# Weight splits at a higher scheduler priority, and the last head's share last in the first two tiles of the second output product

## The chip, the core and the metric

The kernel runs on one core of one Trainium2 chip. A core has a matrix engine (TensorE, PE in the profile, with its weight loads as PEld), a vector engine (VectorE, DVE), a scalar engine (ScalarE, ACT), GpSimd (POOL) and SyncE (SP), which here issues most DMAs. The metric is the device time of one execution in microseconds.

## The reference

Two blocks of a network, 512 tokens of width 1024, all in float32. Block 1: a hybrid mixer (chunk gating beside a gated delta rule with 4 heads), cross attention to 256 memory tokens, an MLP with squared ReLU. Block 2: a mixer with an mLSTM and a sliding-window attention, an MLP, and a gate with per-layer inputs. What matters here, cut to its core:

```python
h = rmsnorm(x, norm_mix)
y_a = chunk_spatial_gating(gu, gv, ...)             # 512 columns
o = gated_delta_rule(q, k, v, g, beta)              # 4 heads x 128
o = rmsnorm(o, dn_onorm) * silu(gate)
x = x + concatenate([y_a, o]) @ w_out               # w_out: 1024 x 1024
x = x + memory_cross_attention(rmsnorm(x, norm_xa), rmsnorm(mem, norm_mem), ...)
x = x + squared_relu_mlp(rmsnorm(x, norm_mlp), ffn_w1, ffn_w2)
```

## The kernel before

Activations lie feature-major in SBUF: 8 tiles of 128 features x 512 tokens (`x`, x_fm in the profile). TensorE multiplies float32 operands as two shorter parts, hi and lo: `mm3` issues three matmuls for one product, hi x hi (L276), hi x lo (L277) and lo x hi (L278). In a feature-major product the weights are the fixed operand, 128 x 128, and 512 tokens stream.

Weights come in pieces of 128 x 1024 through `wload` (L249): a DMA on SP into a raw buffer (wr, 2 of them), a cast to hi on ScalarE (L257, wh) and a subtraction raw − hi on VectorE (L258, wl; 3 buffers each of wh and wl). A raw buffer is free for the next DMA when the subtraction has read it, and a wh buffer for the next cast when TensorE has done its last matmul with it. `wgran` loads the two pieces that a product with 1024 rows needs; `w_out_b`, with 512 rows, needs one. In the two MLPs there are extra buffers (wrx, whx, wlx), and there the second product's weights come through `st_weights` and `split_sb` (casts in L318, subtractions in L319), not through `wload`. `split_sb` is also what splits activations: hi on ScalarE (L321 with a scale), lo on VectorE (L322).

No order is written by hand. A scheduler goes through the program once, and puts each engine's instructions into one fixed list by priority and by what is ready in its own plan; the priority goes by the place in the program. On the chip each engine runs its list in that order, and an instruction whose data isn't there holds up the rest of its list.

Four places are spoken of below.

- **The last head** (at about 285 us in the profile). Each delta-rule head ends in `fin`: four transposes (L768, tile c) and a `split_sb` into `yb` (L321, L322). `w_out1` multiplies the four heads' `yb` by `w_out_b`: `g` goes over four pieces of weights, each with two output tiles (PSUM tiles psd), and each tile adds up the four heads, k = 0 to 3 (`proj_fm`). Behind each tile stands `ev`: the residual (L465) and the norm's split and squares.
- **The memory projections** (150 to 285 us). The norm of the memory tokens and the projections `xa_wk` and `xa_wv` run beside the delta rule's heads. The heads' triangular solves are groups of small matmuls (L656) with small rows on VectorE between them.
- **From the first MLP to mixer 2** (765 to 795 us). The MLP's last products end in PSUM tiles x and are added to x_fm (L977). A norm follows: split and squares (L321, L322, L331, L332), the sum over features by matmuls with a column of ones (`tok_rs`: L340 into pss, L342), an inverse root in 11 small rows on VectorE (`rsqrt`, L180 to L185, three Newton steps), a second one, and `tok_bc` (L349 copies, TensorE transposes in L352, ScalarE copies in L354). Mixer 2's first tiles don't need the result in their matmuls, only in their evacuation.
- **From the second MLP to the tail** (1615 to 1640 us). The same norm, with one inverse root.

## Time and profile before

| | us |
|---|---|
| median of 3 runs | 1704.14 (1703.59 to 1705.08) |
| the profiled execution's own time | 1704.19 |
| its span, first to last instruction | 1702.4 |
| TensorE busy | 1678.3 |
| VectorE busy | 1214.9 |
| ScalarE busy | 821.8 |

The times are of whole executions; the profile is of one. What the kernel's trace records lies within the span, and 1.8 us of the execution's time lie around it. A matmul's busy time includes the pipeline's depth, so two matmuls in a row overlap: what one costs is read from the distance of two starts, and what a wait costs from the same distance less the usual one. In a row of the timeline stand the start, the duration, the engine, the line, the operation, out <- in and shape, and in brackets the idle time ahead of it with what ended it. In a row of windows stand the window, its length, busy time of PE, PEld, DVE, ACT and POOL with their counts, the granted clock, the share of the DMA engines and GB/s.

### The profile page before, as it was taken

Reading aid. Unit: us, or ns where it says so; the run is one execution under the profiler, and the core shown is the slowest. Engines: PE = TensorE matmul, PEld = TensorE weight load, DVE = VectorE, ACT = ScalarE, POOL = GpSimd, SP = SyncE. Lnnn points to the kernel's source line nnn. Section 1 sums busy time; section 2 is a strip of 40 time slices with the busy share of each in tenths; the row PEclk is TensorE's granted clock in tenths of the full one; section 3 lists DMA queues with packets and bytes.
Section 4 is the critical chain, followed back from the end, with each engine's and each line's share of the span. In section 5 each row is a group of like instructions: output and inputs, shape, how many; then the busy total and the mean of one; then the engine's idle time right before and its main releaser. Section 6 shows DMA issues by size and latency. Waiting matters only on the chain.

```text
span 1702.4 us, 25975 instructions
## 1 busy us (share of the span) xinstructions
PE 1678.3 (99%) x9924; PEld 1453.7 (85%) x9924; DVE 1214.9 (71%) x2574; ACT 821.8 (48%) x1462; POOL 66.2 (4%) x86
## 2 busy tenths in 40 slices
PE   9999999999999999999999999999999999999998
PEld 8988888887898989898988887788888989898987
DVE  6988885656676768688845569865556767676875
ACT  6365745444444444454444457654244444444553
POOL 0200000000000000000000000000000000000000
PEclk9999999999999999999999999999999999999999
DMA  6321367545545464423333332334464454643331
GB/s 203 100 76 54 94 160 176 136 99 169 124 137 161 136 161 136 124 89 110 101 94 93 100 87 72 90 87 123 112 189 127 133 165 132 166 133 121 100 112 50
DMA packets 81948, 205.64 MB, mean 121 GB/s; under 512 B 13088, under 2 KB 14240, under 8 KB 81824
## 3 DMA queue, kind: packets, MB, share of 16 engines
q1 hardware_dynamic: 62672, 169.29, 31.8%
q0 software_dynamic: 9216, 16.78, 6.7%
q10 hardware_dynamic: 9936, 17.91, 3.8%
q8 instruction: 78, 1.28, 0.3%
q14 instruction: 46, 0.38, 0.1%
HBM read 201.59 MB, written 35.65 MB: 139 GB/s over the span
## 4 chain that ended last, share of the span: by engine, by line
PE 88%; DVE 8%; ACT 2%; issue 1%; DMA 1%; ACTq 0%; DVEq 0%
PE psd L277 21%; PE psd L278 21%; PE psd L276 21%; PE x L276 5%; PE x L277 5%; PE x L278 5%; DVE wl L258 2%; PE c L656 1%; PE c L602 1%; ACT wh L257 1%; PE lg L1338 1%; PE po L1365 1%; DVE acc L332 1%; DVE S L432 1%; PE m L1259 1%
## 5 line engine op out<-in xcount | busy, mean ns | idle before, releaser
L278 PE MATMUL psd<-S,wl 128*128 128x512 f32 (+1 forms) x1256 | 483.9, 386 | 2.6 <-DVE wl L258 2.5
L276 PE MATMUL psd<-S,wh 128*128 128x512 f32 (+1 forms) x1256 | 482.9, 385 | 1.1 <-ACT S L321 1.1
L277 PE MATMUL psd<-S,wh 128*128 128x512 f32 (+1 forms) x1192 | 458.9, 385 | 1.0 <-DVE S L322 0.8
L278 PEld LDWEIGHTS psd<-S,wl 128*128 128x128 f32 x1256 | 236.3, 188 | 48.0 <-DVE wl L258 3.8
L276 PEld LDWEIGHTS psd<-S,wh 128*128 128x128 f32 x1256 | 236.6, 188 | 46.4 <-ACT S L321 1.5
L258 DVE TENSOR_TENSOR wl<-wr,wh 128x1024 fp32r<-128x1024 f32 (+2 forms) x160 | 192.1, 1200 | 115.1 <-ACT wh L257 113.1
L277 PEld LDWEIGHTS psd<-S,wh 128*128 128x128 f32 x1192 | 224.3, 188 | 44.1 <-DVE S L319 1.4
L257 ACT CAST wh<-wr 128x1024 fp32r<-128x1024 f32 (+2 forms) x160 | 163.9, 1026 | 151.5 <-PE psd L277 104.9
L278 PE MATMUL psd<-wh,S 128*128 128x256 f32 (+2 forms) x480 | 135.8, 283 | 0.0
L276 PE MATMUL psd<-wh,S 128*128 128x256 f32 (+2 forms) x480 | 135.6, 283 | 0.0
L277 PE MATMUL psd<-wl,S 128*128 128x256 f32 (+2 forms) x480 | 135.5, 282 | 0.0
L276 PE MATMUL x<-S,wh 128*128 128x256 f32 x452 | 128.0, 285 | 3.3 <-DVE x_fm L977 2.9
L277 PE MATMUL x<-S,wh 128*128 128x256 f32 x452 | 126.4, 281 | 0.0
L278 PE MATMUL x<-S,wl 128*128 128x256 f32 x452 | 126.0, 280 | 0.0
L277 PE MATMUL psd<-S,whx 128*128 128x512 f32 (+1 forms) x296 | 109.0, 368 | 0.1
L276 PE MATMUL psd<-S,whx 128*128 128x512 f32 (+1 forms) x296 | 107.9, 366 | 0.0
L278 PE MATMUL psd<-S,wlx 128*128 128x512 f32 (+1 forms) x296 | 107.1, 362 | 0.0
L977 DVE TENSOR_TENSOR x_fm<-x_fm,x 128x256 f32<-128x256 f32 x192 | 78.8, 416 | 27.2 <-PE x L278 27.0
L276 PEld LDWEIGHTS psd<-wh,S 128*128 128x128 f32 x480 | 90.4, 189 | 0.4
L277 PEld LDWEIGHTS psd<-wl,S 128*128 128x128 f32 x480 | 90.4, 188 | 0.4
L278 PEld LDWEIGHTS psd<-wh,S 128*128 128x128 f32 x480 | 90.5, 188 | 0.1
L276 PEld LDWEIGHTS x<-S,wh 128*128 128x128 f32 x452 | 84.9, 188 | 6.4 <-DVE x_fm L977 3.2
(465 smaller groups left out, 3178.7 us busy)
## 6 DMA issues: line engine op xcount, KB each, us to landing
wrx<-in_ffn_w_dram SPq DMA_DIRECT2D x32, 512.0 KB
wrx<-in_w_up_dram SPq DMA_DIRECT2D x20, 512.0 KB
wr<-in_w_in_qk_dram SPq DMA_DIRECT2D x16, 512.0 KB
sums_ffn_w<-in_ffn_w_dram ACTq DMA_DIRECT2D x32, 256.0 KB
wr<-in_ffn_w_dram SPq DMA_DIRECT2D x16, 512.0 KB
sums_w_down<-in_w_down_dram ACTq DMA_DIRECT2D x32, 256.0 KB
wr<-in_w_in_v_dram SPq DMA_DIRECT2D x12, 512.0 KB
wr<-in_w_up_dram SPq DMA_DIRECT2D x12, 512.0 KB
```

The source lines that it names most:

```text
L257: self.last_cast = nc.scalar.copy(hi[:, c], raw[:, c])
L258: nc.vector.tensor_tensor(out=lo[:, c], in0=raw[:, c], in1=hi[:, c].bitcast(F32), op=ALU.subtract)
L276: mm(ps, ah, bh, start=first, stop=False, skip_group_check=more)
L277: mm(ps, ah, bl, start=False, stop=False, skip_group_check=more)
L278: self.last_mm = mm(ps, al, bh, start=False, stop=last, skip_group_check=more)
L332: nc.vector.tensor_tensor(out=acc, in0=acc, in1=sq, op=ALU.add)
L432: nc.vector.tensor_scalar(out=d, in0=d, scalar1=ag[:, j, 0:1], scalar2=r[:, j:j + 1], op0=ALU.subtract, op1=ALU.mult)
L602: nc.tensor.matmul(blk(ps, b), lhs(b), rhs(b), start=True, stop=True)
L656: nc.tensor.matmul(ps[:, b * n:(b + 1) * n], lhs[:, b], rhs(b), start=True, stop=True)
L977: TT(out=x[n][t], in0=x[n][t], in1=ps, op=op)
L1259: nc.tensor.matmul(pX[:, :W], PT[:, tt], va[:, tt], start=True, stop=True)
L1338: nc.tensor.matmul(ps[:, i, K0:], qs[:, 2 * e2 + i, cs], kd[:, w, kc], start=(w == 0), stop=(w == 1))
```

## The change

The cast and the subtraction of every piece of weights that comes through `wload` get a priority that is higher by 400. The scheduler may so place them earlier in ScalarE's and VectorE's lists; the DMA that fills the raw buffer keeps its own. `split_sb` returns its cast. The cast of the second piece of `w_out_b` (g = 1) must be issued after head 3's cast. In `w_out1` the two tiles of the first piece are opened together: k = 0, 1, 2 of both, then k = 3 of both, then both evacuations. No arithmetic is added or removed.

```diff
@@ -246,7 +246,7 @@
                 lambda: self.t(p, [P, kt, n], "wl" + x, F32R, bufs=b))
 
 
-    def wload(self, src, kt, n, pieces=None):
+    def wload(self, src, kt, n, pieces=None, behind=None):
 
         nc = self.nc
         raw, hi, lo = (f() for f in self.wtiles(kt, n))
@@ -254,18 +254,20 @@
             nc.sync.dma_start(raw[:, c], src[:, c])
             if then:
                 then()
-            self.last_cast = nc.scalar.copy(hi[:, c], raw[:, c])
-            nc.vector.tensor_tensor(out=lo[:, c], in0=raw[:, c], in1=hi[:, c].bitcast(F32), op=ALU.subtract)
+            with self.tc.high_priority(400):
+                with self.tc.issue_after(behind.ins) if behind else nullcontext():
+                    self.last_cast = nc.scalar.copy(hi[:, c], raw[:, c])
+                nc.vector.tensor_tensor(out=lo[:, c], in0=raw[:, c], in1=hi[:, c].bitcast(F32), op=ALU.subtract)
         return hi, lo
 
-    def wgran(self, name, g, n=256, nk=8, pieces=None):
+    def wgran(self, name, g, n=256, nk=8, pieces=None, behind=None):
 
         if self.wx is None:
             self.job()
         src = self.D[name]
         parts = []
         for h in range(nk // 4):
-            parts.append(self.wload(src[g, h], 4, n, pieces if h == 0 else None))
+            parts.append(self.wload(src[g, h], 4, n, pieces if h == 0 else None, behind))
         hi = [parts[k // 4][0][:, k % 4] for k in range(nk)]
         lo = [parts[k // 4][1][:, k % 4] for k in range(nk)]
         return hi, lo
@@ -315,11 +317,12 @@
 
         nc = self.nc
         if scale is None:
-            nc.scalar.copy(hi, src)
+            cast = nc.scalar.copy(hi, src)
             nc.vector.tensor_tensor(out=lo, in0=src, in1=hi.bitcast(F32), op=ALU.subtract)
         else:
-            nc.scalar.activation(hi, src, AF.Copy, scale=scale)
+            cast = nc.scalar.activation(hi, src, AF.Copy, scale=scale)
             nc.vector.scalar_tensor_tensor(out=lo, in0=src, scalar=scale, in1=hi.bitcast(F32), op0=ALU.mult, op1=ALU.subtract)
+        return cast
 
     def sq_acc(self, acc, src, k, scale=None, n=T):
         nc = self.nc
@@ -766,7 +769,7 @@
             psy = psc()
             for b in range(NB):
                 nc.tensor.transpose(blk(psy, b), o[:, b], ident)
-            self.split_sb(yb_h[:, h], yb_l[:, h], psy, self.vec[:, C_ONORM:C_ONORM + 1])
+            self.yb_cast = self.split_sb(yb_h[:, h], yb_l[:, h], psy, self.vec[:, C_ONORM:C_ONORM + 1])
 
         yield fin
 
@@ -780,8 +783,19 @@
             self.add_res(o, ps)
             self.norm_tile(o, xh, xl, acc, "norm_xa")
 
-        for g in range(4):
-            self.proj_fm(self.wgran("w_out_b", g, nk=4), *self.yb, (2 * g, 2 * g + 1), ev)
+
+        wh, wl = self.wgran("w_out_b", 0, nk=4)
+        (yh, yl), ps = self.yb, [self.psd() for _ in range(2)]
+        for ks in ((0, 1, 2), (3,)):
+            for j in range(2):
+                for k in ks:
+                    c = slice(j * P, (j + 1) * P)
+                    self.mm3(ps[j], wh[k][:, c], wl[k][:, c], yh[k], yl[k], k == 0, k == 3)
+        for j in range(2):
+            ev(j, ps[j])
+        for g in range(1, 4):
+            w = self.wgran("w_out_b", g, nk=4, behind=self.yb_cast if g == 1 else None)
+            self.proj_fm(w, *self.yb, (2 * g, 2 * g + 1), ev)
         self.dump("x1", self.x)
         return xh, xl, acc
```

The lines of the rows below are those of each kernel's own file: from `wload` on, a line of the changed kernel is some 2 to 14 higher (L258 becomes L260, L321 and L322 become L323 and L324, L768 becomes L771, L977 becomes L991).

**The last head.** ScalarE's list before, from the scale of head 3's output (do) by its norm. wh_3580 is the second piece of `w_out_b`; S_176_1229 is `yb`, split from the transposed head (c_619_3448); S_592_3235 belongs to the memory projections.

```order
L763 ACTIVATE do_2947<-do_2947,dsc_2996 128x128 x4
L257 CAST wh_3580<-wr_3579 128x1024
L321 ACTIVATE S_176_1229<-c_619_3448,vec 128x512
L321 ACTIVATE S_592_3235<-psd_3496,rsmy_2723 128x256
L219 DMA sums_ffn_w_5_68<-in_ffn_w_dram 128x512
L257 CAST wh_3626<-wr_3625 128x1024
L219 DMA sums_ffn_w_5_68<-in_ffn_w_dram 128x512
```

And of the changed kernel, at the same place:

```order
L766 ACTIVATE do_2947<-do_2947,dsc_2996 128x128 x4
L323 ACTIVATE S_592_3235<-psd_3496,rsmy_2723 128x256
L323 ACTIVATE S_176_1229<-c_619_3448,vec 128x512
L259 CAST wh_3580<-wr_3579 128x1024
L259 CAST wh_3626<-wr_3625 128x1024
L219 DMA sums_ffn_w_5_68<-in_ffn_w_dram 128x512 x2
L323 ACTIVATE S_628_3528<-x_fm,vec 128x512
```

Head 3's cast now stands ahead of the second piece's cast. On TensorE, the list before around head 3's transposes (L768); psd_3496 is the last tile of the memory projections and psd_3541 the first of `w_out1`, with wh_3536 the first piece of `w_out_b`:

```order
L768 MATMUL c_619_3448<-masks,do_2947 128x128
L276 MATMUL psd_3496<-wh_3464,S_477_2660 128x256
L768 MATMUL c_619_3448<-masks,do_2947 128x128
L277 MATMUL psd_3496<-wl_3465,S_477_2660 128x256
L278 MATMUL psd_3496<-wh_3464,S_478_2661 128x256
L276 MATMUL psd_3496<-wh_3464,S_477_2660 128x256
L277 MATMUL psd_3496<-wl_3465,S_477_2660 128x256
L278 MATMUL psd_3496<-wh_3464,S_478_2661 128x256
L276 MATMUL psd_3541<-S_176_1229,wh_3536 128x512
```

and in the changed kernel, where psd_3542 is the second tile of `w_out1`:

```order
L279 MATMUL psd_3541<-S_177_1230,wh_3536 128x512
L771 MATMUL c_619_3448<-masks,do_2947 128x128 x2
L280 MATMUL psd_3541<-S_176_1229,wl_3537 128x512
L771 MATMUL c_619_3448<-masks,do_2947 128x128
L278 MATMUL psd_3541<-S_176_1229,wh_3536 128x512
L771 MATMUL c_619_3448<-masks,do_2947 128x128
L279 MATMUL psd_3541<-S_177_1230,wh_3536 128x512
L280 MATMUL psd_3541<-S_176_1229,wl_3537 128x512
L278 MATMUL psd_3541<-S_176_1229,wh_3536 128x512
L279 MATMUL psd_3541<-S_177_1230,wh_3536 128x512
L280 MATMUL psd_3541<-S_176_1229,wl_3537 128x512
L278 MATMUL psd_3542<-S_176_1229,wh_3536 128x512
```

The transposes have moved from the end of the memory projections into the first products of `w_out1`. Before, five matmuls of psd_3496 and nine of psd_3541 (k = 0 to 2) stand between the last transpose and the first matmul that needs head 3 (k = 3); now it is 14 of the two tiles of `w_out1`, and all six matmuls of k = 3 come behind them.

**From the first MLP to mixer 2.** VectorE's list before, from L342, where the row sums of the norm are read; rsi, rsy and rst are the inverse root's tiles, and wl_8182 is a piece of mixer 2's weights:

```order
L342 TENSOR_SCALAR rsv_8018<-pss_8013 128x4
L258 TENSOR_TENSOR wl_8182<-wr_8180,wh_8181 128x1056
L180 TENSOR_SCALAR rsi_8020<-rsv_8018 128x4
L1202 MEMSET mprev_8494 128x4
L181 TENSOR_SCALAR rsy_8021<-rsi_8020 128x4
L183 TENSOR_TENSOR rst_8022<-rsy_8021 128x4
L184 SCALAR_TENSOR_TENSOR rst_8022<-rst_8022,rsv_8018 128x4
L185 SCALAR_TENSOR_TENSOR rsy_8021<-rst_8022,rsy_8021 128x4
L183 TENSOR_TENSOR rst_8022<-rsy_8021 128x4
L184 SCALAR_TENSOR_TENSOR rst_8022<-rst_8022,rsv_8018 128x4
L185 SCALAR_TENSOR_TENSOR rsy_8021<-rst_8022,rsy_8021 128x4
L183 TENSOR_TENSOR rst_8022<-rsy_8021 128x4
```

and in the changed kernel, where wl_8188 and wl_8303 are the next two pieces:

```order
L260 TENSOR_TENSOR wl_8188<-wr_8186,wh_8187 128x1056
L345 TENSOR_SCALAR rsv_8018<-pss_8013 128x4
L180 TENSOR_SCALAR rsi_8020<-rsv_8018 128x4
L181 TENSOR_SCALAR rsy_8021<-rsi_8020 128x4
L1216 MEMSET mprev_8494 128x4
L183 TENSOR_TENSOR rst_8022<-rsy_8021 128x4
L184 SCALAR_TENSOR_TENSOR rst_8022<-rst_8022,rsv_8018 128x4
L185 SCALAR_TENSOR_TENSOR rsy_8021<-rst_8022,rsy_8021 128x4
L183 TENSOR_TENSOR rst_8022<-rsy_8021 128x4
L184 SCALAR_TENSOR_TENSOR rst_8022<-rst_8022,rsv_8018 128x4
L185 SCALAR_TENSOR_TENSOR rsy_8021<-rst_8022,rsy_8021 128x4
L260 TENSOR_TENSOR wl_8303<-wr_8301,wh_8302 128x1024
```

Before, wl_8188 stands 5 rows behind the last of these and wl_8303 16 rows. wl_8182 has moved up among the squares, wl_8188 stands ahead of the first row of the inverse root, and wl_8303 behind its second Newton step. On TensorE, 10 more matmuls of mixer 2's first two tiles now stand ahead of the MLP's last products, 48 of which follow them instead of 36, and the row sums come later: 25 matmuls lie between the MLP's last product and the first row sum, where there were 20.

**From the second MLP to the tail.** VectorE's list before; x_15919, x_15920 and x_16049 are PSUM tiles of the MLP's second product, and wlx_16163 belongs to the tail's weights:

```order
L977 TENSOR_TENSOR x_fm<-x_fm,x_15920 128x256
L977 TENSOR_TENSOR x_fm<-x_fm,x_16049 128x256
L258 TENSOR_TENSOR wlx_16163<-wr_16161,whx_16162 128x512
L977 TENSOR_TENSOR x_fm<-x_fm,x_15919 128x256
L322 SCALAR_TENSOR_TENSOR S_2480_15755<-x_fm,vec,S_2478_15753 128x512
L332 TENSOR_TENSOR acc_15756<-acc_15756,sq_16015 128x512
L319 TENSOR_TENSOR wl_16046<-wrx_16024,wh_16045 128x1024
L322 SCALAR_TENSOR_TENSOR S_2480_15755<-x_fm,vec,S_2478_15753 128x512
L332 TENSOR_TENSOR acc_15756<-acc_15756,sq_16020 128x512
L977 TENSOR_TENSOR x_fm<-x_fm,psd_16051 128x256
```

and in the changed kernel, with wlx_16185 the tail's next piece:

```order
L991 TENSOR_TENSOR x_fm<-x_fm,x_15920 128x256
L260 TENSOR_TENSOR wlx_16163<-wr_16161,whx_16162 128x512
L991 TENSOR_TENSOR x_fm<-x_fm,x_15919 128x256
L324 SCALAR_TENSOR_TENSOR S_2480_15755<-x_fm,vec,S_2478_15753 128x512
L335 TENSOR_TENSOR acc_15756<-acc_15756,sq_16015 128x512
L324 SCALAR_TENSOR_TENSOR S_2480_15755<-x_fm,vec,S_2478_15753 128x512
L260 TENSOR_TENSOR wlx_16185<-wrx_16183,whx_16184 128x512
L335 TENSOR_TENSOR acc_15756<-acc_15756,sq_16020 128x512
L321 TENSOR_TENSOR wl_16046<-wrx_16024,wh_16045 128x1024
L991 TENSOR_TENSOR x_fm<-x_fm,x_16049 128x256
```

The residual from x_16049 has moved behind a norm's rows and two subtractions. On TensorE the 12 matmuls that write the next part into x_16049 now come after 12 of x_16050.

## The prediction

> **What bounds the kernel now.** I read the page's first part first, then the costliest groups with the idle time ahead of them, then PE's timeline around every wait of more than 0.3 us, and then what stands on DVE and ACT there.
>
> ```profile
> PE 1678.3 (99%) x9924; PEld 1453.7 (85%) x9924; DVE 1214.9 (71%) x2574; ACT 821.8 (48%) x1462; POOL 66.2 (4%) x86
> PEclk9999999999999999999999999999999999999999
> L278 PE MATMUL psd<-S,wl 128*128 128x512 f32 (+1 forms) x1256 | 483.9, 386 | 2.6 <-DVE wl L258 2.5
> L276 PE MATMUL psd<-S,wh 128*128 128x512 f32 (+1 forms) x1256 | 482.9, 385 | 1.1 <-ACT S L321 1.1
> L277 PE MATMUL psd<-S,wh 128*128 128x512 f32 (+1 forms) x1192 | 458.9, 385 | 1.0 <-DVE S L322 0.8
> L258 DVE TENSOR_TENSOR wl<-wr,wh 128x1024 fp32r<-128x1024 f32 (+2 forms) x160 | 192.1, 1200 | 115.1 <-ACT wh L257 113.1
> ```
>
> PE is busy for 1678.3 of the 1702.4 us of the span, at full clock, so all its idle time is 24.1 us and the change can't pay more than that. The three groups show how little of it the change aims at: PE waited 2.5 us for a subtraction of weights, and 1.1 + 0.8 us for the two halves of a split of S, 4.4 us in all, or 0.26% of the time. The subtraction takes 1.20 us on DVE, 160 times; none is added or removed. Everything is a matter of order: what the sooner weights save, and what they push back on DVE and ACT, which run their rows in the order shown above.
>
> **The last head.**
>
> ```profile
> 289.12 0.40 PE L278 MATMUL psd<-S,wl 128*128 128x512 f32 x1
> 290.58 0.50 PE L276 MATMUL psd<-S,wh 128*128 128x512 f32 x1 [1.06 <-ACT S L321]
> 291.92 0.50 PE L277 MATMUL psd<-S,wh 128*128 128x512 f32 x1 [0.84 <-DVE S L322]
> 292.25 0.39 PE L278 MATMUL psd<-S,wl 128*128 128x512 f32 x1
> 292.48 0.39 PE L276 MATMUL psd<-S,wh 128*128 128x512 f32 x1
> ...
> 288.90 1.05 ACT L257 CAST wh<-wr 128x1024 fp32r<-128x1024 f32 x1 [2.44 <-DMA wr<-in_w_out_b_dram]
> 289.85 0.68 ACT L321 ACTIVATE S<-c,vec 128x512 fp32r<-128x512 f32 x1
> ...
> 289.98 1.22 DVE L258 TENSOR_TENSOR wl<-wr,wh 128x1024 fp32r<-128x1024 f32 x1 [4.90 <-ACT wh L257]
> 291.12 0.74 DVE L322 SCALAR_TENSOR_TENSOR S<-c,vec,S 128x512 fp32r<-128x512 f32 x1
> ```
>
> Two starts of 128x512 matmuls lie 0.23 us apart (292.25 to 292.48). The three matmuls of k = 3 wait first for head 3's cast, which stands on ACT behind the cast of the next weights, and that one waits 2.44 us for its DMA; then for head 3's subtraction, behind the weights' subtraction. From start to start this costs 290.58 − 289.12 − 0.23 = 1.23 and 291.92 − 290.58 − 0.23 = 1.11, together 2.34 us. In the new order the cast stands ahead of the next weights' cast, and from the last transpose to k = 3 PE has 14 matmuls of 0.23 us, 3.2 us, in which the split needs 0.68 + 0.74 = 1.42 us. Both waits go; with 0.37 us of a wait ahead of the transposes the term is at most −2.7 us. What is late next are the two evacuations, some three matmuls (0.7 us) later; PE's next tiles need them no sooner than the third PSUM buffer, so I cost that at 0. I take **−2.4 us**, between −2.7 and −1.2 (one of the two waits stays).
>
> **The memory projections beside heads 2 and 3.**
>
> ```profile
> 215.96 0.36 PE L277 MATMUL psd<-S,wh 128*128 128x256 f32 x1
> 217.49 0.39 PE L278 MATMUL psd<-S,wl 128*128 128x256 f32 x1 [1.16 <-DVE wl L258]
> 222.98 0.28 PE L277 MATMUL psd<-S,wh 128*128 128x256 f32 x1
> 224.14 0.39 PE L278 MATMUL psd<-S,wl 128*128 128x256 f32 x1 [0.88 <-DVE wl L258]
> 224.48 0.97 PE L656 MATMUL c<-dTb,dT 128*128 128x32 f32 x8
> 226.69 0.97 PE L656 MATMUL c<-dY,dV 128*128 128x32 f32 x8
> ...
> 209.78 1.04 ACT L257 CAST wh<-wr 128x1024 fp32r<-128x1024 f32 x1
> ...
> 216.22 1.21 DVE L258 TENSOR_TENSOR wl<-wr,wh 128x1024 fp32r<-128x1024 f32 x1
> ```
>
> The first wait is for a subtraction whose cast was ready at 210.8 but which DVE took up at 216.22, behind head 3's small rows; from start to start it costs 217.49 − 215.96 − 0.12 = 1.41, and the second 1.04 us. At the higher priority these two subtractions stand 81 and 31 rows earlier, so up to −2.45 us. Against it: the memory norm's rows on DVE and the head's are pushed back by them, and PE's new order puts the groups of L656 closer together. Before, 11 matmuls of 0.12 us lay between the two groups at 224.48 and 226.69 and covered 1.3 us of DVE's work between them; that cover is partly gone. The page shows no such uncovered wait, so I bound it by 0 and by the 1.3 us of cover at two places, 2.6 us. By the nearest row, the one piece of cover that the order clearly takes away, I take half the gain, **−1.0 us**, with ends −2.45 and +0.2.
>
> **From the first MLP to mixer 2.**
>
> ```profile
> 770.95 0.39 PE L277 MATMUL psd<-S,wh 128*128 128x512 f32 x1
> 771.60 0.39 PE L276 MATMUL x<-S,wh 128*128 128x256 f32 x1 [0.26 <-DVE x_fm L977]
> 775.85 0.29 PE L278 MATMUL x<-S,wl 128*128 128x256 f32 x1
> 790.77 0.28 PE L278 MATMUL psd<-wh,S 128*128 128x264 f32 x1
> 791.66 0.63 PE L352 MATMUL pss<-masks,e 128*128 128x128 f32 x4 [0.61 <-DVE e L349]
> ...
> 781.62 0.16 DVE L342 TENSOR_SCALAR rsv<-pss 128x4 f32<-128x4 f32 x1 [0.61 <-PE pss L340]
> 785.39 0.16 DVE L1046 TENSOR_TENSOR rs2v<-rs2v,rsy 128x4 f32<-128x4 f32 x1
> 791.09 0.43 DVE L349 COPY e<-rs2y 128x512 f32<-128x512 f32 x1
> ...
> 787.95 1.05 ACT L257 CAST wh<-wr 128x1024 fp32r<-128x1024 f32 x1 [1.70 <-PE psd L277]
> ```
>
> Here the weights are not what is late. The MLP's last matmul starts at 775.85; then a serial chain runs on DVE (residual, squares, two inverse roots) until L349 at 791.09, and PE fills these 15 us with mixer 2's first tiles. It runs out at 790.77 and waits 0.77 us. In the new order 10 matmuls of 0.23 us, 2.3 us, of those tiles stand ahead of the MLP's last products. The 0.42 us at 771.60 go, and the chain starts 1.9 us later, at about 777.9. Then weights' rows stand in it. wl_8182 is among the squares: the sums, ready at 781.62 − 0.61 = 781.0 before, are ready 1.9 + 1.2 later, at about 784.1. wl_8188 is ahead of L342, which then starts at 785.3. Its small rows take 0.2 us each: from 781.62 to 785.39 there are 13 of them and one subtraction. Two Newton steps are thus done at 787.1, and there wl_8303 stands. Its cast must wait until PE is done with the buffer of wh_8102, as it did 1.70 us before 787.95; PE's last matmul with it now comes behind both groups of row sums (0.9 us each) and nine matmuls (2.1 us), 784.1 + 3.9 = 788.0. A cast and a subtraction later it is 790.2, 3.1 us after DVE got there, of which 1.2 stood in the chain before. The other 18 rows put L349 at about 793.7 instead of 791.09. PE now runs out 0.42 us earlier and waits 0.77 + 2.6 + 0.42 = 3.8 us; what the program loses is L349's delay, **+2.6 us**. The ends: −1.2 (both waits go) and +3.1 (the 1.9 and one more subtraction in the chain).
>
> **From the second MLP to the tail.**
>
> ```profile
> 1619.40 0.75 DVE L977 TENSOR_TENSOR x_fm<-x_fm,x 128x256 f32<-128x256 f32 x2
> 1625.55 0.36 PE L276 MATMUL x<-S,wh 128*128 128x256 f32 x1 [0.91 <-DVE x_fm L977]
> 1629.73 0.28 PE L278 MATMUL x<-S,wl 128*128 128x256 f32 x1
> 1632.63 0.40 PE L276 MATMUL psd<-S,whx 128*128 128x512 f32 x1
> 1633.47 1.02 PE L340 MATMUL pss<-ones,acc 128*128 128x1 f32 x8 [0.45 <-DVE acc L332]
> ```
>
> The second row of the pair at 1619.40 evacuates x_16049. In the new order two more residuals, the four rows of a norm, two subtractions of 0.6 us and wl_16046 (1.2) come ahead of it, 5.5 us of rows after 1619.4: it ends at about 1625.3 instead of 1620.1. Before it PE has 12 matmuls of 0.12 us fewer to do than before its wait now, so it runs dry 1.4 us sooner, at 1625.55 − 0.91 − 1.4 = 1623.2; from 1625.6 on it has 48 matmuls instead of 36, which end at 1631.3 instead of 1629.85: +1.5. After that wl_16282 stands among the last squares, so the row sums of L340 start at about 1636.1; PE has 12 matmuls of 0.23 us until then, and waits 2.0 instead of 0.6 us. Together 1636.1 − 1633.47 less the two matmuls more that are done by then, 0.5: **+2.1 us**, between −1.6 (both waits go) and +2.6.
>
> **What is left.** Mixer 2's attention is where DVE is fullest:
>
> ```profile
> 1000.00:1100.00 100.00, 98.16 (x494) 75.63 (x492) 88.63 (x288) 72.51 (x178) 2.44 (x3) 1.00 0.27 73
> ```
>
> PE is idle for 1.84 of these 100 us. Five subtractions move ahead of softmax rows, and PE's rows are rearranged with them. That can gain 1.84 us at most; it can lose one subtraction, 1.2 us, at two places where a head's matmuls follow directly. The nearest row is DVE's 88.6%, which leaves room for one: **+0.2 us**, a sixth of it, between −1.8 and +2.4.
>
> **Sum.** −2.4 − 1.0 + 2.6 + 2.1 + 0.2 = +1.5 us, on the profiled execution's own 1704.19 us (span 1702.4 and 1.8 around it; 0.05 over the median of the runs): **1705.7 us**, no change that a measurement can tell, since that takes about 0.2%, 3.4 us.
>
> **Rivals.** *The chains hold nothing up* (faster, 0.22). Both inserted norms stand beside PE work of 15 us, and the order is only an order: where casts come sooner, wl_8188 and wl_8303 cost their 1.2 us of a chain that contained them before. Then both ends of an MLP stay at 0 and both aims are met: 1704.2 − 2.4 − 2.4 − 0.4 = 1699.0. For it: the 2.5 and 1.9 us in the first groups. Against it: the buffer wait of 1.70 us at 787.95, which no order on DVE takes away.
>
> *A subtraction blocks DVE behind a cast that waits for PE's buffer* (slower, 0.18). It is the mechanism of wl_8303: DVE stops at that row until PE has released the buffer. It decides as soon as the release comes later than the chain gets there; in the sum that is the wait of 0.9 us ahead of wl_8303's cast. If it acts in the tail's wlx_16185 and in the attention too, and the memory term is 0: 1704.2 − 2.4 + 3.1 + 2.6 + 2.4 = 1709.9.
>
> *The clock falls in the longer wait* (slower, 0.08). The trace shows the granted clock fall once, at the end:
>
> ```profile
> 1697.09 0.65 PE L1450 MATMUL psd<-masks,x_fm 128*128 128x128 f32 x4 [3.04 <-ACT S L1453]
> 1698.00:1699.00 1.00, 0.00 (x0) 0.00 (x0) 0.00 (x0) 0.47 (x1) 0.00 (x0) 0.50 1.00 377
> ```
>
> A wait of 3.04 us, 0.65 us of work, and the clock is 0.50. The wait that I expect at 790.5 is 3.8 us. If the clock is then at half for as long as that wait, half of that time is lost, or all of it if the work that takes as long at full clock is slowed: +1.9 to +3.8, 1705.7 + 2.8 = 1708.5. Against it: PE had worked again by then, so the row doesn't say that the wait alone does it. The Trainium skill, page "TensorE: Matmul & The Clock Gate", Part 1, says that the clock is halved after an idle window of about 3.4 us that runs freely, and stays so for such a window of work; the row at the end agrees with the half, and by that rule the price would be 1.7 us, an estimate.
>
> *It doesn't do what it says* (same, within the forecast's 0.52): the casts come sooner in order, but the raw weights don't land sooner, as the 2.44 us at 288.90 show. Then the memory term is 0: 1706.7.
>
> **Numbers.** Forecast 0.52 (1702.2 to 1707.6, some half of each term's ends), unhurt transitions 0.22, blocking 0.18, the clock 0.08. The forecast's own width stays within 0.2%, and the rivals lie beyond it, so faster 0.22, same 0.52, slower 0.26. The range for 8 in 10 goes from 1700.0, which leaves out the better half of the first rival, to 1710.0, the second's time.
>
> **What would show it.** Right: no wait above 0.3 us between 285 and 293; PE waiting more than 3 us for L349 near 790, and about 2 us for the row sums near 1633. Wrong: those two waits below 1 us, or new waits for softmax rows between 1000 and 1100 that add up to more than 2 us.

## The result, and the profile after

| | before | changed |
|---|---|---|
| median, us | 1703.91 (1703.59 to 1705.08, 4 runs) | 1724.85 (1724.13 to 1726.68, 4 runs) |
| ratio | 1 | 1.0118 [1.0106, 1.0131] |
| span of the profiled execution, us | 1702.4 | 1722.9 |
| mean granted TensorE clock in it | 0.999 | 0.991 |

The change makes the kernel slower by 1.2%, 20.9 us. The forecast was 1705.7, no change; the time lies far above its range.

From the page of the changed kernel: engines, the granted clock in 40 slices, and the four groups that were shown of before (busy time and mean ns, then the idle time just before them and what ended most of it).

```profile
PE 1691.2 (98%) x9924; PEld 1464.2 (85%) x9924; DVE 1218.9 (71%) x2574; ACT 820.8 (48%) x1462; POOL 66.5 (4%) x86
PEclk9999989999999999999999999999999999999999
L280 PE MATMUL psd<-S,wl 128*128 128x512 f32 (+1 forms) x1256 | 485.6, 387 | 0.5 <-DVE wl L260 0.5
L278 PE MATMUL psd<-S,wh 128*128 128x512 f32 (+1 forms) x1256 | 484.2, 386 | 0.9 <-DVE x_fm L468 0.8
L279 PE MATMUL psd<-S,wh 128*128 128x512 f32 (+1 forms) x1192 | 459.6, 386 | 0.7 <-DVE S L324 0.5
L260 DVE TENSOR_TENSOR wl<-wr,wh 128x1024 fp32r<-128x1024 f32 (+2 forms) x160 | 191.7, 1199 | 113.3 <-ACT wh L259 111.8
```

Two things are to be seen. The waits that the change aimed at are gone: 0.5 us for weights' subtractions instead of 2.5. And TensorE, with the same 9924 matmuls, is busy for 12.9 us longer than before; one slice of the clock shows an 8. TensorE's idle time has grown too, from 24.1 to 31.7 us (span less busy). So part of the time is waiting, and part is the same work done slower.

The waits, in TensorE's timeline of the changed kernel:

```profile
228.65 0.47 PE L355 MATMUL pss<-masks,e 128*128 128x128 f32 x1 [3.23 <-DVE e L352]
230.36 1.91 PE L659 MATMUL c<-dTb,dT 128*128 128x32 f32 x8 [1.24 <-DVE dTb L685]
315.71 0.47 PE L278 MATMUL psd<-S,wh 128*128 128x512 f32 x1 [0.77 <-DVE x_fm L468]
803.97 1.09 PE L355 MATMUL pss<-masks,e 128*128 128x128 f32 x4 [3.16 <-DVE e L352]
1641.93 0.38 PE L278 MATMUL x<-S,wh 128*128 128x256 f32 x1 [2.39 <-DVE x_fm L991]
1652.80 0.95 PE L278 MATMUL psd<-S,whx 128*128 128x512 f32 x3 [1.26 <-ACT S L320]
```

There are three places: the memory stage (228), the start of mixer 2 (804), the start of the tail (1642). The row at 230.36 says more than its wait: the group of eight L659 matmuls takes 1.91 us, where it took 0.97 at 224.48 before. The windows of the granted clock (length, busy us of PE, PEld, DVE, ACT, POOL with their counts, clock, DMA share, GB/s), first two windows of the changed kernel inside the memory stage and the one that holds all of its fall, then the falls at the two other places:

```profile
226.00:228.00 2.00, 0.00 (x0) 0.00 (x0) 1.79 (x12) 0.00 (x0) 0.00 (x0) 0.64 0.83 121
228.00:230.00 2.00, 0.47 (x1) 0.18 (x1) 0.53 (x3) 0.00 (x0) 0.00 (x0) 0.50 0.38 41
226.00:245.00 19.00, 15.02 (x72) 13.96 (x73) 10.02 (x37) 5.34 (x12) 0.00 (x0) 0.55 0.18 28
803.00:811.00 8.00, 6.36 (x31) 5.99 (x32) 6.10 (x14) 2.78 (x5) 0.00 (x0) 0.57 0.01 2
1643.00:1647.00 4.00, 4.00 (x24) 4.00 (x23) 1.11 (x2) 0.62 (x1) 0.00 (x0) 0.57 0.57 166
```

and the memory stage of the kernel before:

```profile
200.00:250.00 50.00, 47.31 (x367) 43.95 (x366) 43.31 (x174) 28.07 (x81) 3.24 (x4) 1.00 0.52 140
```

A clock of 0.55 over 19 us is a half clock for 2 x 0.45 x 19 = 17.1 us. In the same way the others are 6.9 and 3.4 us: five, two and one time 3.4. Before, the clock is 1.00 everywhere until the last wait of the program. Work at half clock costs half of its own time: of the 15.02 us busy in the first stretch some 1.4 come after it has ended, so (15.0 − 1.4) / 2 = 6.8; likewise (6.4 − 0.8) / 2 = 2.8 and 3.4 / 2 = 1.7. By this estimate the clock makes 11.3 of the 20.5 us between the spans; the experiments check the 2.8 and put 1.3 in the place of the 1.7, and no run checks the 6.8.

Where the time is lost, by comparing when TensorE starts its n-th matmul in both traces; the orders differ a little, so a single figure is good to some tenths:

| stretch (time before) | us lost in it | total |
|---|---|---|
| to 215, early part | +2.5 | 2.5 |
| 215 to 280, memory stage | +8.2 | 10.7 |
| 280 to 295, the last head | −2.3 | 8.4 |
| 295 to 322, `w_out1` | +1.8 | 10.2 |
| 322 to 743 | −0.3 | 9.9 |
| 743 to 880, into mixer 2 | +5.5 | 15.4 |
| 880 to 1616 | +0.9 | 16.3 |
| 1616 to 1634, into the tail | +4.2 | 20.5 |

**The memory stage.** VectorE before, from the last square of the memory tokens' norm to the row that TensorE's L352 waits for:

```profile
207.90 0.42 DVE L332 TENSOR_TENSOR acc<-acc,sq 128x256 f32<-128x256 f32 x1
211.26 0.16 DVE L342 TENSOR_SCALAR rsmv<-pss 128x2 f32<-128x2 f32 x1 [0.21 <-PE pss L340]
222.00 0.29 DVE L349 COPY e<-rsmy 128x256 f32<-128x256 f32 x1
```

and in the changed kernel, with the subtractions from 189 on:

```profile
189.04 1.18 DVE L260 TENSOR_TENSOR wl<-wr,wh 128x1024 fp32r<-128x1024 f32 x1
205.77 1.22 DVE L260 TENSOR_TENSOR wl<-wr,wh 128x1024 fp32r<-128x1024 f32 x1
213.50 1.20 DVE L260 TENSOR_TENSOR wl<-wr,wh 128x1024 fp32r<-128x1024 f32 x1
217.43 0.41 DVE L335 TENSOR_TENSOR acc<-acc,sq 128x256 f32<-128x256 f32 x1
218.37 1.23 DVE L260 TENSOR_TENSOR wl<-wr,wh 128x1024 fp32r<-128x1024 f32 x1
221.46 1.21 DVE L260 TENSOR_TENSOR wl<-wr,wh 128x1024 fp32r<-128x1024 f32 x1
223.38 0.14 DVE L345 TENSOR_SCALAR rsmv<-pss 128x2 f32<-128x2 f32 x1
228.30 0.30 DVE L352 COPY e<-rsmy 128x256 f32<-128x256 f32 x1
```

Five subtractions run between 189 and 223, ahead of the row sums' reading. Before, one ran from 189 to the reading at 211.26 (at 203.32), and two more between the reading and the copies (216.22 and 219.44); so by the copies it is five instead of three. The last square comes 9.5 us later, the reading of the row sums 12.1, the copies 6.3. TensorE is itself only 2.5 us later there, and its order is fixed: from 226 to 228 it does nothing at all.

**Mixer 2.** VectorE of the changed kernel, from the inverse root on:

```profile
795.53 0.17 DVE L181 TENSOR_SCALAR rsy<-rsi 128x4 int32<-128x4 int32 x1
797.60 0.15 DVE L183 TENSOR_TENSOR rst<-rsy 128x4 f32<-128x4 f32 x1 [1.90 <-issue]
797.62 0.06 DVE L1216 MEMSET mprev<- 128x4 f32 x1
798.69 1.23 DVE L260 TENSOR_TENSOR wl<-wr,wh 128x1024 fp32r<-128x1024 f32 x1
803.39 0.43 DVE L352 COPY e<-rs2y 128x512 f32<-128x512 f32 x1
```

wl_8303, the last subtraction here, came without a wait. What held the chain up is the 1.90 us ahead of the memset of mprev, which stands in the list just ahead of L183. In the fixed order that row waits for TensorE, and TensorE's second group of row sums (0.94 us from 796.61 on) ends just then:

```profile
796.61 0.94 PE L1057 MATMUL pss<-ones,acc 128*128 128x1 f32 x8
```

The memset starts 0.07 us after this group's end in each of three traces: at 797.62 here, at 783.25 before, and at 788.70 in the run e8 below, where the group comes elsewhere; so it is this group that releases it. Before, the group started 1.6 us behind the first one (782.23 and 780.62) and ended just as the chain came to the memset; now 2.8 us lie between the two groups (796.61 and 793.85), since mixer 2's matmuls stand between them.

**The tail.** VectorE of the changed kernel, ahead of the residual that TensorE waits for at 1641.93:

```profile
1639.13 0.69 DVE L260 TENSOR_TENSOR wlx<-wrx,whx 128x512 fp32r<-128x512 f32 x1
1640.33 1.22 DVE L321 TENSOR_TENSOR wl<-wrx,wh 128x1024 fp32r<-128x1024 f32 x1
1641.47 0.74 DVE L991 TENSOR_TENSOR x_fm<-x_fm,x 128x256 f32<-128x256 f32 x2
```

A raised subtraction and, behind it in the list, wl_16046 stand ahead of the residual, as the order shown with the change has it.

### The profile page after: what moved, and what is told of

Same layout as the page of the kernel before. It is cut to its first block, busy times and chain, and to the rows that moved or that the text cites. A ratio compares the mean times of both kernels' runs of the same rounds, so it can differ in the third digit from the quotient of the medians.

```text
span 1722.9 us, 25999 instructions
## 1 busy us (share of the span) xinstructions
PE 1691.2 (98%) x9924; PEld 1464.2 (85%) x9924; DVE 1218.9 (71%) x2574; ACT 820.8 (48%) x1462; POOL 66.5 (4%) x86
## 4 chain that ended last, share of the span: by engine, by line
PE 85%; DVE 9%; ACT 3%; issue 1%; DMA 1%; SPq 0%; ACTq 0%; DVEq 0%
PE psd L279 20%; PE psd L280 20%; PE psd L278 20%; PE x L278 5%; PE x L279 5%; PE x L280 5%; DVE wl L260 2%; PE c L659 1%; ACT wh L259 1%; PE c L605 1%; DVE acc L335 1%; PE po L1379 1%; DVE S L324 1%; PE lg L1352 1%; DVE S L435 1%
## 5 line engine op out<-in xcount | busy, mean ns | idle before, releaser
L260 DVE TENSOR_TENSOR wl<-wr,wh 128x1024 fp32r<-128x1024 f32 (+2 forms) x160 | 191.7, 1199 | 113.3 <-ACT wh L259 111.8
L991 DVE TENSOR_TENSOR x_fm<-x_fm,x 128x256 f32<-128x256 f32 x192 | 78.8, 415 | 30.8 <-PE x L280 30.5
```

The lines of the kernel that those rows point to most:

```text
L260: nc.vector.tensor_tensor(out=lo[:, c], in0=raw[:, c], in1=hi[:, c].bitcast(F32), op=ALU.subtract)
L991: TT(out=x[n][t], in0=x[n][t], in1=ps, op=op)
```

## The experiments

Theory A: the raised priority puts weights' subtractions into serial chains on VectorE at three places; TensorE runs dry there; and in each of these waits the granted clock falls and stays low after it. The rival at first: the new order in `w_out1` is what costs, or the waits cost only their own length and the clock is an accompaniment. Times below are medians, a ratio is to the kernel before in runs beside them on the same chip, and "clock" is the granted one.

**Each half of the change alone.** First the priority without the new `w_out1`, then the new `w_out1` at the old priority:

```diff
+        for g in range(4):
+            self.proj_fm(self.wgran("w_out_b", g, nk=4), *self.yb, (2 * g, 2 * g + 1), ev)
```

```diff
-            with self.tc.high_priority(400):
+            with nullcontext():
```

> The higher priority as in the changed kernel, the second output product as before. Theory A (the priority is the loss: it makes PE wait at three places, beside heads 2 and 3, at mixer 2's start and at the tail's, and the granted clock falls behind each): all three waits and falls stay, the 2 us of the last head come back, 1726 to 1728 us. Theory B (the reordered output product and its wait are the loss): 1703 to 1705 us.

> The reordered second output product with the wait for head 3's cast, without the higher priority. Theory A: none of the three new waits, clock 1.00 throughout, the two waits of 1.06 and 0.84 us at the last head gone, 1701.0 to 1702.5 us. Theory B: 1720 us or more.

Priority only: 1726.95 us, ratio 1.0138 [1.0121, 1.0155], with waits of 3.23, 1.09, 3.15 and 2.40 us at the three places. New order only: 1702.64, ratio 0.9992 [0.9983, 1.0001], clock 1.00 until the last wait. So the whole loss belongs to the priority. The new order does what it says: both waits of the last head are gone, which brings TensorE 2.4 us forward at 289, but 1.3 of it is given back by 322, above all here:

```profile
315.24 0.50 PE L279 MATMUL psd<-S,wh 128*128 128x512 f32 x1 [0.80 <-DVE S L324]
```

In the priority-only kernel the wait at the tail is as long as in the changed one, and the clock does not fall there:

```profile
1643.12 0.39 PE L278 MATMUL x<-S,wh 128*128 128x256 f32 x1 [2.40 <-DVE x_fm L981]
1643.00:1647.00 4.00, 3.88 (x31) 3.75 (x32) 1.84 (x5) 0.62 (x1) 0.00 (x0) 1.00 0.40 141
```

From there the price of the clock at the tail can be read: the 240 matmuls from the one that starts at 1616 before take 44.2 us before, 47.1 here and in e3 (below) with this wait and no fall, and 48.4 to 48.5 in the changed kernel and in e4 and e6, where the wait is the same and the clock falls. The two longer waits cost 2.9 us, the fall 1.3.

Why the clock falls in one and not in the other can be read from the traces. In each of the 17 traces all changes of the clock ahead of the program's last wait lie whole multiples of 3.413 us apart; in the changed kernel the falls begin at 226.55, 803.40 and 1643.08, which is 169 and then 246 such steps apart. So the clock changes only at the borders of windows of 3.413 us, which run on whatever the program does. The window ahead of the changed kernel's fall at the tail, and the two over which the same wait is spread with the priority only:

```profile
1639.67:1643.08 3.41, 1.15 (x10) 1.15 (x11) 2.87 (x6) 0.50 (x1) 0.00 (x0) 1.00 0.63 166
1638.69:1642.10 3.41, 2.04 (x18) 1.82 (x16) 3.41 (x6) 2.62 (x4) 0.00 (x0) 1.00 0.83 275
1642.10:1645.51 3.41, 2.39 (x18) 2.26 (x19) 2.18 (x6) 0.62 (x1) 0.00 (x0) 1.00 0.61 204
```

The first holds the whole wait and matmuls of 2320 columns in all (the columns are the last number of a matmul's shape); the others hold 4057 and 4608. A window of 128x512 matmuls in a row, 0.23 us each, holds 7550. Counted so over all traces, from 12 us to 1690, 29 windows at full clock are followed by half clock, and each of them holds 2951 columns or fewer; of the 8234 that are not, three hold fewer (records of matmuls can be missing). At half clock, windows with 2752 and fewer are followed by half clock, those with 2794 and more by full clock. So it is neither a wait's length nor TensorE's busy time alone that decides, but how much a window of 3.4 us streams: under some 2750 to 2950 columns, not quite two fifths of what is possible, the clock is at half in the next one. This is a reading across all traces; no run was built to test it.

**The priority taken back place by place.** A flag leaves the ordinary priority to the weights of one stage: of the two memory projections (e3), of the first pieces of mixer 2 and of the tail (e5), of all weights ahead of `w_out1` (e6), of e5 and e6 together (e7).

```diff
-            with self.tc.high_priority(400):
+            with self.tc.high_priority(400) if self.pri else nullcontext():
```

> The changed kernel, but the pieces of xa_wk and xa_wv at the ordinary priority. By the two traces the stretch from 200 to 245 us costs 7.7 us. Theory A: the wait of 3.23 us and the fall of the clock behind it go, 1716 to 1718.5 us, with the losses at mixer 2 and the tail as they are. Rival C (the loss is that of one chain of weights and shifts to the next stage): 1723 us or more.

> The changed kernel, but the weights of mixer 2's first head (w_in_qk2, w_in_o0, w_in_v2) and of the whole tail at the ordinary priority. By the two traces mixer 2's start costs 5.0 us and the tail's 4.3. Theory A (subtractions of weights inside the norm's chain, then the clock): both go, the waits are again 0.6 and 0.9 us, the clock is 1.00 there, 1715 to 1716.5 us. Rival C (the loss shifts to the next place where weights stand ahead of a chain): 1720 us or more.

> The changed kernel, but all weights ahead of the second output product at the ordinary priority. Up to there the changed kernel loses 10.8 us by the count of matmuls. Leaving out the memory's weights alone gave back 3.3 of them, and the clock then fell 3 us later, at the same solve of head 2. Theory A': any weights that push the solve's or the norm's rows back start the same fall, so all must be left out: clock 1.00 in 200 to 250 us, 1713 to 1715 us. Rival E (the last head's reordered product is part of this loss): 1718 us or more.

> Both of the two before in one: the higher priority stays for the second output product, cross attention, both MLPs and mixer 2 from its second head on. Theory A': the losses of the two add up and are gone, 1702.5 to 1705 us (the reorder alone took 1702.6), clock 1.00 up to the last wait. Rival C: 1710 us or more, with a wait of over 2 us at some third place.

| | median, us | ratio | half-clock stretches ahead of the last wait, us |
|---|---|---|---|
| changed kernel | 1724.85 | 1.0118 [1.0106, 1.0131] | 17.1, 6.9, 3.4 |
| e3 | 1721.56 | 1.0105 [1.009, 1.0121] | 13.7, 6.8 |
| e5 | 1715.48 | 1.0065 [1.005, 1.008] | 17.1 |
| e6 | 1713.02 | 1.0056 [1.0037, 1.0075] | 6.8, 3.4 |
| e7 | 1704.24 | 1.0 [0.999, 1.0009] | none |

The stretches are those of the profiled executions; of e7's ten runs one took 1710.34 us, at a clock of 0.994.

e5, e6 and e7 came out as expected: by the medians the two later transitions are worth 9.4 us, the early weights 11.8, and without both nothing is lost. Nothing is won either. e3 is a miss, 3 us too slow: with the memory projections at the ordinary priority the norm's wait goes, but others come in the same stage, and the clock falls there as before:

```profile
227.22 0.39 PE L282 MATMUL psd<-S,wl 128*128 128x256 f32 x1 [1.48 <-DVE wl L262]
200.00:250.00 50.00, 47.07 (x314) 43.47 (x315) 38.26 (x149) 26.06 (x80) 2.44 (x3) 0.86 0.39 95
```

So the memory projections' own rows don't do it alone; the other weights ahead of `w_out1`, which e6 takes back too, have their part.

**Keeping TensorE busy in the wait.** Matmuls whose result nobody reads are put into the wait: 31 in the memory norm's (e4), 21 in mixer 2's (e10). VectorE's chains stay as they are; what changes is only whether TensorE idles.

In mixer 2, ahead of its second `tok_bc`:

```diff
+            nc.tensor.matmul(ps[:, 8:12], self.mask("ident"), v, start=True, stop=True)
+            for _ in range(20):
+                nc.tensor.matmul(ps[:, 256:512], xh[0][:, 0:P], xh[1][:, 0:256], start=True, stop=True)
```

> The changed kernel with 31 matmuls more, whose result nobody reads, put on PE while the memory norm's inverse root runs (from L345 on), 30 of them 128x256 at 0.12 us, 3.5 us. If the fall of the clock is what costs most at this place (theory A), the clock stays at 1.00 between 220 and 245 us and the time falls by 4 to 6 us, to 1719 to 1721, although PE has more to do. If the wait itself is the price (rival D), the time stays at 1725 or rises by up to 3 us.

> The changed kernel with 21 matmuls more, whose result nobody reads, put on PE in mixer 2's wait (20 of them 128x256, 2.4 us, behind the row L1061 at 800.8 us). The wait for L352 stays as long, but PE works through most of it. If the clock's fall is a price of its own (theory A), the clock stays at 1.00 from 795 to 815 us, and the stretch that now costs 5.0 us costs 2.7 to 3.2: 1722 to 1723.5 us in all. If the wait alone is the price (rival D), the stretch still costs 5 us, 1725.

In mixer 2 it is clean. The wait is filled, the clock stays up, from TensorE's timeline and the window around it:

```profile
801.67 2.63 PE L1066 MATMUL pss<-S 128*128 128x256 f32 x20
804.36 0.66 PE L355 MATMUL pss<-masks,e 128*128 128x128 f32 x4
795.00:815.00 20.00, 19.43 (x149) 18.38 (x149) 16.14 (x50) 7.05 (x12) 0.00 (x0) 1.00 0.26 67
```

From the end of a 1.70 us wait for x_fm at 769 (the kernel before has it too, at 759) to the group of L1309 at 867, TensorE takes 98.24 us in the changed kernel and 95.46 here. So of the 5.5 us that are lost between 743 and 880 the clock makes 2.8, and the late chain the other 2.7. In all, 1721.24 us, ratio 1.0102 [1.0084, 1.012], a little under the range expected by theory A. In the memory stage theory A's expectation was missed, and the run is inconclusive: 1723.21, ratio 1.0114 [1.0099, 1.013]; the wait is filled, and the clock falls all the same, 6 us later at 232.84, for 13.65 us. So an idle stretch of 3 us is not needed in that stage: no wait of TensorE between 200 and 250 is over 0.7 us there.

**Late chains without early weights, and the reverse.** On the kernel with only the new order, additions with no use are put on VectorE ahead of the memory norm's reading of the row sums, 9 (3.7 us, e13) or 4 (1.7 us, e14): the norm is late, the weights are where they were. And on the changed kernel the norms' own rows get a still higher priority, 800 (e8); the same 400 for the norms alone, with ordinary weights, is e9.

The additions in the norm's `tok_rs`, and the priority of 800 around `tok_rs`, `tok_bc` and mixer 2's second inverse root:

```diff
+        for _ in range(delay):
+            w = self.t(self.tp, [P, 256], "sq")
+            last = nc.vector.tensor_tensor(out=w, in0=acc, in1=acc, op=ALU.add)
```

```diff
+        with self.tc.high_priority(800):
```

> The reordered product with ordinary weights, and nine additions of 128x256 (0.4 us each, 3.7 us, results unread) ahead of the memory norm's first row on VectorE: what the higher priority did to that norm (5.5 us later than PE's row sums), without the weights. If lateness of the norm is the cause (theory A), PE waits beside heads 2 and 3 and the clock falls in most runs: 1707 to 1713 us, single runs far apart. If it needs the weights themselves (rival I): 1703 to 1705 us.

> The same with four additions, 1.7 us. Theory A: the clock falls in some runs and not in others; 1703 to 1709 us. Rival I: 1702.5 to 1704 us.

> The changed kernel, with the norms' chains (row sums, inverse roots, broadcast) at a priority higher by 800, above the weights. In its order the memory norm's row sums are read at row 490 instead of 513 of VectorE's list, but two subtractions stand in the chain, and at mixer 2's start the order stays almost as it is (three subtractions in the chain). Theory A: it is the place in the list that counts: the memory norm's wait of 3.23 us shrinks to below 1.5, 1717 to 1722 us, and mixer 2's wait of 3.16 us stays. Rival F (what holds the norm up is the DMA or PE, not VectorE's list): 1724 to 1726 us.

> The reordered second output product with ordinary weights, and the norms' chains (row sums, inverse roots, broadcast) at a priority higher by 400. In its order wl_8182 and wl_8188 still stand in mixer 2's chain, since that is when they are ready; the memory norm comes 19 rows sooner. Theory A: places that wait for a chain gain a little, 1701 to 1703 us, clock 1.00 up to the last wait. Rival H (the chains' small rows push other work back, as the weights did; the chains at 800 above the weights lost 3 us ahead of 200 us): 1704 to 1708 us.

e13: 1722.41 us, ratio 1.0111 [1.0096, 1.0126]. 3.7 us of rows cost 19.8 against the kernel they were added to, 9 us more than the expected range allowed:

```profile
221.84 0.58 PE L280 MATMUL psd<-S,wl 128*128 128x256 f32 x1 [3.34 <-DVE wl L260]
269.12 1.92 PE L664 MATMUL c<-dTb,dT 128*128 128x32 f32 x8 [2.86 <-DVE dTb L690]
200.00:250.00 50.00, 45.85 (x282) 42.59 (x281) 37.60 (x149) 24.06 (x72) 2.44 (x3) 0.80 0.38 97
```

e14: 1711.65, ratio 1.0048 [1.0031, 1.0066], 9.0 us for 1.7 us of rows, again more than expected. No long wait is there at all, and still a half clock for 2 x 0.14 x 50 = 14 us:

```profile
217.89 0.38 PE L280 MATMUL psd<-S,wl 128*128 128x256 f32 x1 [1.29 <-DVE wl L260]
224.48 0.38 PE L280 MATMUL psd<-S,wl 128*128 128x256 f32 x1 [0.97 <-DVE wl L260]
200.00:250.00 50.00, 46.88 (x312) 42.83 (x311) 39.77 (x164) 24.86 (x75) 2.44 (x3) 0.86 0.42 113
```

So lateness on VectorE in this stage is enough; that it came from weights in the changed kernel doesn't matter. e8 shows the other direction: with the norms ahead of the weights the memory stage's wait and its fall are gone, and the time goes to 1717.38, ratio 1.0083 [1.0066, 1.01], as expected; mixer 2's wait is still 3.04 us, here without a stop at the memset, and with subtractions of weights in the chain at 787.15 and 791.01. e9, the norms alone, came to 1712.86, ratio 1.0046 [1.0026, 1.0067], over 8 runs from 1705.89 to 1718.26, above both expected ranges: raising the chains is no gain by itself. Why it costs that much stays open; in the profiled execution (1706.59) the clock is low for 3.41 us from 226.10 on.

**A smaller step.** The priority is raised by 20 (e11) and by 40 (e12) instead of 400.

> The changed kernel with a priority higher by 20 instead of 400. In its order only single pieces move: wl_2754 stands ahead of the memory norm's first row (row 473 instead of 507), both transitions are as in the kernel before. Theory A: no wait over 2 us, no fall of the clock before the last, 1701 to 1703.5 us (the reordered product's gain, and perhaps the 1.4 us of the first memory wait). Rival G (any higher priority of weights costs, in proportion to what moves): 1704 to 1708 us.

> The same with 40: four memory pieces move, the first two by 10 and 79 rows, the norm's first row stands at 486 instead of 473, both transitions as before. Theory A: the norm comes later, but a wait of 1 to 2 us doesn't let the clock fall; 1701 to 1705 us. Rival G: 1706 to 1712 us.

1710.0 us, ratio 1.0021 [1.0007, 1.0036], and 1707.97, ratio 1.0025 [1.001, 1.0039], of 12 runs each. Theory A's expectation was missed in both; 40 came out in rival G's range, 20 above it. In the profiled execution of e11 one wait in the memory stage is 2.04 us long, and the clock falls for 6.8. The runs of one kernel fall into two groups: those with a mean clock of 0.996 and more take 1703 to 1707 us, those with 0.991 to 0.994 take 1709 to 1715. The profiled execution of e11, with its fall of 6.8 us, belongs to the first (1704.81, 0.997), that of e12, with a fall of 13.65, to the second (1710.89, 0.994). How long the clock is low, then, is not decided by the program alone; since the windows run on by themselves, the place of their borders differs from run to run. The kernel before is not far from that edge: of 25 of its runs on that chip one took 1709.24 us, at a clock of 0.994, where the others had 0.997 and more.

**What a pause costs in dense work.** On the kernel with only the new order, six pauses are forced upon TensorE between products of `w_br_a` and `w_br_b`, far from the three places: a tiny matmul, n small rows on VectorE, and a tiny matmul that waits for them.

```diff
+        nc.vector.tensor_copy(v, ps[:, 0:4])
+        for _ in range(n):
+            nc.vector.tensor_tensor(out=v, in0=v, in1=v, op=ALU.mult)
+        return nc.tensor.matmul(ps[:, 8:12], ident, v, start=True, stop=True)
```

> The reordered product with ordinary weights, and six pauses of PE in dense 128x512 work (between the column pairs of w_br_a and w_br_b, some 11 us of matmuls after each): PE waits for a chain of 4, 9, 14 and 6, 11, 16 small VectorE rows of 0.2 us, about 1.5, 2.5, 3.5 and 1.9, 2.9, 3.9 us. This measures the price of a wait by itself. Theory J (windows of 3.41 us that run freely, judged by how much of them PE worked): the pauses below 2 us never let the clock fall, those of 3.5 and 3.9 us always or nearly always, those of 2.5 and 2.9 sometimes; each fall lasts 3.41 us and costs 1.5 to 1.7 us beside the wait. Theory K (the fall needs a wait of a fixed length, 3.4 us): only the 3.5 and 3.9 us pauses fall, each time. Total: 1702.6 + 16.2 of pauses + 2 to 4 falls = 1722 to 1726 us.

1746.29 us, ratio 1.0254 [1.0236, 1.0271]. The pauses came out longer than planned, 3.69 to 6.02 us, and so the time was missed by 20 us. The shortest and the longest, with the clock around each:

```profile
1183.39 0.38 PE L326 MATMUL pss<-pz,masks 128*128 128x4 f32 x2 [3.69 <-DVE pz L325]
1269.82 0.59 PE L326 MATMUL pss<-pz,masks 128*128 128x4 f32 x2 [6.02 <-DVE pz L325]
1180.00:1190.00 10.00, 6.61 (x23) 5.32 (x24) 2.97 (x12) 0.43 (x1) 0.81 (x1) 0.83 0.46 128
1262.00:1278.00 16.00, 9.98 (x34) 7.99 (x33) 6.63 (x22) 1.66 (x2) 0.00 (x0) 0.68 0.22 66
```

Half clock for 2 x 0.17 x 10 = 3.4 us and for 2 x 0.32 x 16 = 10.2. All six pauses made the clock fall, for 3.4, 3.4, 3.4, 6.8, 6.8 and 10.2 us. The pauses add up to 28.2 us, the half clock to 34.1, of which 5.5 lie within the pauses: 28.2 + (34.1 − 5.5) / 2 = 42.5, against 43.65 measured over the kernel without them. So the price of a fall, half of the low stretch that holds work, is confirmed by itself. From what length on a pause lets the clock fall this run can't tell, since all six were over 3.6 us. By the count of columns above, and as an estimate, a window of dense work must lose some 2.1 us (1 − 2950 / 7550, of 3.41): a shorter wait is harmless there, and one between 2.1 and 4.2 us falls or doesn't by where it lies on the windows.

No version beats both kernels: the new order alone is 0.08% under the kernel before, with an interval that touches 1.

## Why the prediction was wrong

- **The bound.** That TensorE was full at full clock, and that 24.1 us of idle time were all that could be won, was right. What was left out is that the full clock was itself something to lose.
- **The last head, −2.4.** Right in its place: −2.4 in the kernel with the new order alone, −2.3 in the changed one, and no wait above 0.3 us between 285 and 293. The step that costed the two later evacuations at 0 was wrong: with the new order alone 1.3 us come back in `w_out1`'s next tiles, in waits for x_fm and for the split, and of the 1.8 us in the changed kernel 0.9 is such a wait.
- **The memory projections, −1.0 (−2.45 to +0.2).** This is the step that failed. The two waits for weights did go, as priced. But against them the prediction set only "the one piece of cover that the order clearly takes away", between the groups of L656. It said that the norm's rows "are pushed back" and did not follow that chain to the copies that TensorE waits for. Followed, it is four more subtractions of 1.2 us ahead of the reading of the row sums, five instead of three ahead of the copies, in a stage in which VectorE was 43.31 of 50 us busy. The wait of 3.23 us came from there: with the norms put ahead of the weights (e8) it is gone. And the term put the clock at nothing: behind that wait it was at half for 17.1 us, some 6.8 of the +8.2 us measured by the estimate above. No run with the late chain kept the clock up in this stage, so how the two share the loss is not shown.
- **Mixer 2, +2.6.** The forecast wait of 3.8 us came as 3.16, and the chain costs 2.7 us without the clock, as the run with the filled wait shows. The size was right, the cause that was named was not: VectorE stood for 1.90 us ahead of the memset, and not at wl_8303. That the sizes agree is luck.
- **The tail, +2.1.** Right in place and kind; the waits cost 2.9. The first is for the residual from x_16049, as forecast, and with 2.39 us it is as long as forecast (1625.6 − 1623.2 = 2.4). The second lies ahead of the split (1.26), where the prediction had put 2.0 at the row sums.
- **Mixer 2's attention, +0.2.** Right: +0.2 between 1000 and 1120 by the count of matmuls.
- **The early part** wasn't priced. It costs 1.3 us by 98 us of the span and 2.5 by 215, in the changed kernel, between 0 and 5 in the others. In the changed kernel 0.8 of it arises at 34.09, where TensorE waits 1.06 us for the first norm's copies (0.20 before, at 33.77): in that chain a subtraction of weights at 31.05 held VectorE up for 0.78 us until its cast was done. In the others up to 2 us are there by 10 us, where the clock at the program's start becomes full at different times: the first 128x512 matmuls take 0.63 us until 10.4 in the kernel with the priority only, and 0.39 from 6.3 on before. The rest stays open.
- **The rival of the clock, +2.8, with a chance of 0.08.** The mechanism was right, and its price at mixer 2 came out at 2.8 too; that is partly luck, since it was worked out from the length of the wait, 3.8 us, and the clock was low for two windows, 6.8 us, of which 5.6 held work. It was thought of at one place only, and of little weight because "the row doesn't say that the wait alone does it". It acted at three: 6.8 (estimated) + 2.8 + 1.3 us. Without these 10.9 the loss between the spans would be 9.6 us instead of 20.5.

The prediction quoted the Trainium skill, page "TensorE: Matmul & The Clock Gate", Part 1: the clock is halved after an idle, freely running window of about 3.4 us, and is full again after one busy window. The runs agree on the window and on its running freely: ahead of the last wait every low stretch is a multiple of 3.41 us, and all its borders lie on one grid of 3.413 us. They differ twice: 2.39 us of idle time suffice where the page asks for a whole window, and beside the delta rule's heads the clock stayed low for five windows in which TensorE was busy for some 13.6 of 17.1 us. The count of columns fits both: 2320 in the tail's window, and at most 2148 in each of the first four of those five.

## What to carry to other kernels

Before work is raised in a scheduler's order, look up which serial chains share its engine, and follow each chain to the row that the bounding engine waits for, with every raised row that now stands ahead of it; the waits that the raise removes are the smaller part. Where the bounding engine is TensorE at full clock, price a new wait of 2 to 3 us at its length and half of one or two low windows more, 1.3 to 2.8 us here, and at up to 7 us, by estimate, in a stage of small matmuls that leans on VectorE. In dense work a filler that keeps TensorE streaming through such a wait was worth the clock's part of it; in the stage of small matmuls it was not. The granted clock by stage is the first view to read of a kernel that became slower with the same work.

## What the runs showed of the hardware that was not expected

- The granted clock falls for whole multiples of 3.41 us: 3.4, 6.8, 10.2, 13.65 and 17.1 us were seen, also 20.5 in e13. Within a trace all its changes lie on one grid of 3.413 us.
- In the memory stage, where small matmuls of 32 columns alternate with groups of 128x256, waits of 1.29 and 0.97 us sufficed for a fall of 13.65 us in e14, while the kernel with the new order only had 1.16 and 0.87 us at the same two places and kept its clock. The window of 3.41 us ahead of e14's fall holds 2496 columns, that of the other kernel, from 222.75 on, 3059. Over all traces the edge lies between 2750 and 2960 columns of at most some 7600; of 8338 windows two lie on the wrong side of it, with 1870 and 2601 columns and the clock full behind them.
- The same kernel, on the same chip, runs with falls of different length: 1703 to 1707 us with 6.8 us or less (as far as profiled), and 1709 to 1715 us, in the kernels with the small step.
- A memset of 0.06 us held VectorE up for 1.90 us while it waited for a group of matmuls, and the profile calls that wait "issue".
